# A two-layer encoder kernel on one core: layer 0's Fourier projection without the fold, q's norm moved into the masked minimum, roots by power, and another share of the PSUM banks

## The chip, the cores and the metric

The kernel runs on one core of a Trainium2 chip. The metric is the device time in microseconds (us) of one launch. The kernel before took 1091.9 us, the median of three runs (1090.97 to 1093.92).

## What is computed

Two layers over 512 positions of 1024 channels, in float32. Cut to what matters, each layer does this:

```python
h = rmsnorm(x, norm1[l])
p = h @ w_in[l]                       # columns: u (512) | q (8 x 64) | k (2 x 64) | v (2 x 64)
y_f = real(fft2(u, norm="ortho")) @ w_fourier[l] + b_fourier[l]
q = rope(rmsnorm(q, q_norm[l]));  k = rope(rmsnorm(k, k_norm[l]))
y_a = windowed_gqa(q, k, v, sink[l])  # |i - j| <= 128, a sink logit per head, blocks of 128 queries
x = x + concat(rmsnorm(y_f, g_fourier_out[l]), rmsnorm(y_a, g_attn_out[l])) @ w_o[l]
h = rmsnorm(x, norm2[l])
up = dwconv3(h @ w_up[l]);  gate, val = halves of up      # 2 x 2816 columns
x = x + (silu(gate) * val) @ w_down[l]
```

The real part of a two-dimensional Fourier transform is cosines over positions and channels less sines over both. Cosine columns are even and sine columns odd, so a transform of 512 points can be taken on sums and differences of mirrored points: 257 even values and 255 odd ones. This is called the fold here.

## The kernel before, in words

**Numbers.** Every float32 operand of a matmul is split into a high part, which ScalarE rounds, and a low part, the rest, which VectorE subtracts (`split`, L94, its lines L97 to L101 using the helpers L86, L89 and L92). A product is then three matmuls on TensorE (`mm3`, L106 to L108: high by high, low by high, high by low). x is held transposed, channels on partitions, in eight tiles `x` of 128 x 512.

**A layer's front.** `col_rstd` (L205) sums squares over the channels with eight small matmuls (L209, two columns wide) and calls `rsqrt` (L192): a shift and a subtraction for a first value and three Newton steps, twelve small VectorE operations (L196 to L202). The result r1 has one value for each position, on partitions. `row_rstd` (L212) spreads such values along rows with L216 (128 x 128 matmuls) and one ScalarE copy; the result is called rb.

- QKV: 2 groups x 8 channel tiles x 4 position blocks, each an `mm3` of 384 columns. Group 1 holds q's last pair of heads (called pair 3), k and v; group 0 holds q's pairs 0 to 2. The weights go through `wsplit` in layer 0; for layer 1 the split weights were prepared during layer 0's feed-forward part (`presplit`, L135) and come by DMA (`fetch`, L186). r1 is applied when the sums leave PSUM (L350 to L353).
- The Fourier projection: `fold_h` (L360) scales a tile of x by g and rb1 (L363), folds it (`fold`, L302: one copy of two columns, L304, and two operations of 255 columns) and splits it; in layer 0 `fold_wu` (L308) folds each weight tile too. 120 matmuls of 256 or 258 columns (L509 to L511) make the folded u in four PSUM banks.
- `prep` (L381) makes q and k ready: squares on ScalarE, a sum (L389), the root, a multiplication by the root (L397), rope in three multiplications and an addition, a split. Transposes by TensorE (L423, L434) turn them.
- Two stages of the transform (L529 to L559) with tables from `load_tables` (L272), each evacuated by `stage_out` (L518). The row for the Nyquist term is carried apart (`tail_out`, `altr`, L542 and L544).
- `attention(p)` (L445) for a pair of heads: in 8 blocks, scores into a bank tagged "sc" (L459), a VectorE operation that scales, adds the mask and finds the minimum (L463), an exponential on ScalarE, a reciprocal (L467), a multiplication on GpSimd (L468), transposes (L471), a split, and the products with v (`mm3`). Pair 3 comes first, then 0, then the Fourier output with `fold_wf` (L313) and its norm accF, then pairs 1 and 2.
- Wo in two halves: the first takes the normed Fourier output (`ys`) and is interleaved with attention's last blocks by `issue_after` (L615); the second takes attention's output with the norm accA. An attention's norm is applied to the sums (L636).

**The feed-forward part** is a long row of 512-column matmuls on TensorE, whose sums go through six banks in turn (`FFN_BANKS`).

**What sets the order.** The program is written in the order above, and a scheduler of the framework places the instructions of each engine's queue; a queue runs strictly in its order. Tiles come from rotating pools: a tag names a pool, and its count of buffers says how far a producer may be ahead (`TEMPS`, L72). The eight PSUM banks are shared out by tag (`BANKS`, L71): "mm" 3, "sc" 2, "tp" 2, "av" 1.

## Time and profile before

| | |
|---|---|
| median of three runs | 1091.9 us (1090.97 to 1093.92) |
| the profiled execution | 1089.6 us, its span 1087.8 us |
| granted TensorE clock | 0.995 of full |
| layer 0's front, up to attention's norm | 0 to 171 us |
| layer 0's rest and feed-forward part | to 564 us |
| layer 1's front, up to attention's norm | 564 to 700 us |
| VectorE, ScalarE, GpSimd over the span | 72%, 48%, 8% |

How to read the rows that follow: the page and the answers of the trace name engines PE (TensorE), PEld (its weight loads), DVE (VectorE), ACT (ScalarE), POOL (GpSimd) and SP (the queue that issues DMAs). L106 is line 106 of the kernel. A row of the timeline has the start, the duration, engine, line, operation, the tile written, an arrow and the tiles read, the shape and, behind x, how many of the kind were put together; in brackets stands the idle time before it and what ended it. Tiles whose name begins with ps are PSUM banks. TensorE's durations overlap, since a matmul begins while the one before drains.

### The profile page before, as it was taken

To read this page: it belongs to the slowest core of one execution; us is meant where nothing else is said; L and a number is where in the kernel's file an instruction comes from. 1 tells how busy PE (TensorE), PEld (TensorE's weight loads), DVE (VectorE), ACT (ScalarE), POOL (GpSimd) and SP (SyncE) were. 2 spreads that over 40 slices of the span, in tenths; PEclk is the share of its full clock that TensorE was granted. 3 is DMA by queue.
4 is the path that set the end of the run, shared out by engine and by line. 5 is a ranking of instruction groups with operands and counts; after the bars stand their busy time and mean duration, and the time that the engine had idled before them with its cause. 6 is when DMAs were issued, how large, how long until landed. Compare 5 with 4: busy or idle time off the path is not lost.

```text
span 1087.8 us, 14834 instructions
## 1 busy us (share of the span) xinstructions
PE 1058.9 (97%) x5187; PEld 889.0 (82%) x5187; DVE 785.0 (72%) x1574; ACT 522.4 (48%) x964; POOL 91.0 (8%) x158
## 2 busy tenths in 40 slices
PE   8987999999999999999999999999999999999998
PEld 7866878888888888888899887888888888888887
DVE  7898986787766777777628878386977435787632
ACT  5547863465444454545513676154554223454421
POOL 1014410000000000000000034000210000101000
PEclk9899999999999999999999999999999999999999
DMA  7312442333339943327855421422333333333241
GB/s 248 108 38 64 131 156 78 101 94 97 97 115 341 394 156 97 97 85 268 324 179 189 156 78 39 155 82 95 98 96 92 87 112 97 97 97 97 81 141 51
DMA packets 58573, 141.64 MB, mean 130 GB/s; under 512 B 6521, under 2 KB 19074, under 8 KB 58498
## 3 DMA queue, kind: packets, MB, share of 16 engines
q1 hardware_dynamic: 58498, 140.69, 40.1%
q8 instruction: 41, 0.67, 0.3%
q14 instruction: 34, 0.28, 0.1%
HBM read 117.60 MB, written 23.07 MB: 129 GB/s over the span
## 4 chain that ended last, share of the span: by engine, by line
PE 85%; DVE 10%; DMA 2%; ACT 2%; issue 2%; POOL 0%; SPq 0%; DVEq 0%; ACTq 0%; POOLq 0%
PE ps L106 27%; PE ps L108 27%; PE ps L107 27%; DVE tA L463 1%; DVE act L89 1%; DVE wlo L89 1%; DMA whi<-kept 1%; PE ps L471 1%; PE ps L459 1%; PE ps L216 1%; DVE tA L89 1%; ACT tA L86 1%; DVE tF L89 1%; PE ps L209 1%; DVE pT L89 0%
## 5 line engine op out<-in xcount | busy, mean ns | idle before, releaser
L86 ACT ACTIVATE whi<-wraw 128x512 fp32r<-128x512 f32 (+1 forms) x296 | 181.6, 616 | 290.9 <-PE ps L108 275.5
L106 PE MATMUL ps<-act,whi 128*128 128x512 f32 x768 | 298.9, 389 | 0.0
L107 PE MATMUL ps<-act,wlo 128*128 128x512 f32 x768 | 298.6, 390 | 0.0
L108 PE MATMUL ps<-act,whi 128*128 128x512 f32 x768 | 297.7, 389 | 0.0
L89 DVE TENSOR_TENSOR wlo<-wraw,whi 128x512 fp32r<-128x512 f32 (+1 forms) x304 | 218.7, 723 | 98.7 <-ACT whi L86 97.1
L108 PEld LDWEIGHTS ps<-act,whi 128*128 128x128 f32 x768 | 144.2, 188 | 29.9
L107 PEld LDWEIGHTS ps<-act,wlo 128*128 128x128 f32 x768 | 144.2, 188 | 29.9
L106 PEld LDWEIGHTS ps<-act,whi 128*128 128x128 f32 x768 | 144.2, 188 | 29.8
L92 DVE SCALAR_TENSOR_TENSOR tF<-tF,pb,tF 128x511 f32<-128x511 f32 x176 | 135.3, 772 | 10.7 <-ACT tF L86 8.0
L89 DVE TENSOR_TENSOR tF<-ps,rb 128x512 f32<-128x512 f32 x104 | 71.2, 689 | 77.2 <-PE ps L108 63.0
L106 PE MATMUL ps<-slab,whi 128*128 128x512 f32 (+2 forms) x228 | 86.7, 381 | 2.2 <-ACT whi L86 1.2
L107 PE MATMUL ps<-slab,wlo 128*128 128x512 f32 (+2 forms) x228 | 85.5, 375 | 0.0
L108 PE MATMUL ps<-slab,whi 128*128 128x512 f32 (+2 forms) x228 | 85.0, 375 | 0.0
L86 ACT ACTIVATE tF<-tF,pb 128x512 f32<-128x512 f32 x88 | 71.8, 816 | 12.0 <-DVE tF L89 3.9
L89 DVE TENSOR_TENSOR x<-x,ps 128x512 f32<-128x512 f32 (+1 forms) x49 | 32.8, 675 | 43.6 <-PE ps L108 43.4
L462 POOL COPY tA<-nsink 128x1 f32<-128x1 f32 x64 | 16.7, 265 | 489.4 <-DMA wraw<-in_w_down_dram 392.5
L89 POOL TENSOR_TENSOR tF<-tF,tF 128x512 f32<-128x512 f32 x22 | 30.2, 1374 | 316.2 <-DVE tF L92 309.2
L468 POOL TENSOR_SCALAR tA<-tA,den 128x256 f32<-128x256 f32 (+1 forms) x64 | 42.3, 665 | 130.9 <-DVE den L467 130.5
L106 PEld LDWEIGHTS ps<-slab,whi 128*128 128x128 f32 x228 | 42.8, 188 | 11.0 <-ACT whi L86 1.6
L107 PE MATMUL ps<-pT,wlo 128*128 128x512 f32 (+1 forms) x132 | 51.0, 386 | 0.0
L108 PE MATMUL ps<-pT,whi 128*128 128x512 f32 (+1 forms) x132 | 50.8, 385 | 0.0
L106 PE MATMUL ps<-pT,whi 128*128 128x512 f32 (+1 forms) x132 | 50.8, 385 | 0.0
(168 smaller groups left out, 1671.7 us busy)
## 6 DMA issues: line engine op xcount, KB each, us to landing
wraw<-in_w_up_dram SPq DMA_DIRECT2D x88, 512.0 KB, 3.5
wraw<-in_w_down_dram SPq DMA_DIRECT2D x32, 512.0 KB, 3.7
kept<-tA SPq DMA_DIRECT2D x56, 256.0 KB, 5.7
whi<-kept SPq DMA_DIRECT2D x28, 256.0 KB, 3.9
wlo<-kept SPq DMA_DIRECT2D x28, 256.0 KB, 2.7
kept<-tA SPq DMA_DIRECT2D x32, 192.0 KB, 2.1
wraw<-in_w_down_dram SPq DMA_DIRECT2D x32, 192.0 KB, 2.9
wraw<-in_w_o_dram SPq DMA_DIRECT2D x8, 512.0 KB, 5.2
```

The costliest lines, as they stand in the source:

```text
L86: return nc.scalar.activation(out, in_, func, **kw)
L89: return (eng or nc.vector).tensor_tensor(out, a, b, op=op)
L92: return nc.vector.scalar_tensor_tensor(out=out, in0=a, scalar=s, in1=b, op0=op0, op1=op1)
L106: nc.tensor.matmul(out, a[0], b[0], start=start, stop=False, **kw)
L107: nc.tensor.matmul(out, a[1], b[0], start=False, stop=False, **kw)
L108: nc.tensor.matmul(out, a[0], b[1], start=False, stop=stop, **kw)
L209: nc.tensor.matmul(pt[:, 2 * b:2 * b + 2], acc[:, b * P:(b + 1) * P], ones2, start=True, stop=True)
L216: nc.tensor.matmul(pt[:, b * P:(b + 1) * P], r[:, b:b + 1].to_broadcast([P, P]), ident, start=True, stop=True)
L459: nc.tensor.matmul(sc[:, :n], qT[p][:, e, i * P:(i + 1) * P], kT[g][:, s, j0 * P:(j1 + 1) * P], start=s == 0, stop=s == 1)
L462: nc.gpsimd.tensor_copy(pr[:, n:n + 1], nsink[:, l, h:h + 1])
L463: nc.vector.tensor_tensor_reduce(out=pr[:, :n], in0=sc[:, :n], in1=mask[:, m0:m0 + n], scale=-1.0 / math.sqrt(HD), scalar=nsink[:, l, h:h ...
L468: nc.gpsimd.tensor_scalar(pr[:, :n], pr[:, :n], den[:, i:i + 1], 1.0, op0=ALU.mult, op1=ALU.mult)
```

## The change

1. **Layer 0's u projection is not folded.** It uses the scaled and split x of QKV (`xg`), positions on partitions, and the weights as they are: 8 channel tiles x 4 position blocks x 3 = 96 matmuls of 512 columns. `fold_scaled` folds u over its channels when it leaves PSUM and applies r1. The fold over positions is left out: stage 0 sums over four blocks of 128 positions with four tables, the third and fourth being the first two with alternating signs, made on ScalarE. Layer 0 no longer calls `row_rstd(r1)`. Before the projection, in the program's order, stand the preparation of all q and attention 3.
2. **Layer 1 keeps the fold**, but `row_rstd(r1)` and the eight folds of x are written behind the preparation of k and of pair 3, not ahead of it.
3. **q's norm** no longer multiplies q: −r/8 of each query takes the place of the constant −1/8 in the scale of the masked minimum, so q's rope doesn't wait for the root.
4. **Roots**: `rsqrt` is one VectorE operation and one power (exponent −0.5) on GpSimd.
5. **Banks and buffers**: "mm" 4 and "sc" 1; "tA" 5 buffers instead of 6; the pool "sq" is gone and squares use "tF". Group 0 of QKV uses the banks sc, tp, tp and av, group 1 the four mm banks.
6. The tables and the folded Fourier weights are cut to 257 and 255 columns that start at a tile's edge (the odd part gets a first row of zeros), the tables come in five loads instead of two, half of each `w_fold` tile is loaded, and its sum and difference are written beside it.
7. In layer 0 attention 0 stands behind the Fourier output, with 1 and 2.

```diff
-FFN_BANKS = ("mm", "mm", "mm", "av", "sc", "sc")
+FFN_BANKS = ("mm", "mm", "mm", "mm", "av", "sc")
-    BANKS = {"mm": 3, "sc": 2, "tp": 2, "av": 1}
-             "tA": (512, 6), "tF": (512, 6), "sq": (512, 2)}
+    BANKS = {"mm": 4, "sc": 1, "tp": 2, "av": 1}
+             "tA": (512, 5), "tF": (512, 6)}
...
     def rsqrt(ssq, n, inv, tag, bufs=2):
         nc.vector.tensor_scalar(v, ssq, inv, EPS, op0=ALU.mult, op1=ALU.add)
-        nc.vector.tensor_scalar(it, v.bitcast(I32), 1, None, op0=ALU.logical_shift_right)
-        nc.vector.tensor_scalar(r.bitcast(I32), it, -1, float(0x5F3759DF), op0=ALU.mult, op1=ALU.add)
-        for _ in range(3):
-            tt(q, r, r, ALU.mult)
-            stt(q, q, -0.5, v, ALU.mult, ALU.mult)
-            stt(r, q, 1.5, r, ALU.add, ALU.mult)
+        nc.gpsimd.tensor_tensor(r, v, mhalf[:, :1].to_broadcast([P, n]), op=ALU.pow)
...
+    def fold_scaled(dst, src, scale):
+        up = temp(256, "tF")
+        act(up[:, :255], src[:, 257:512], scale=scale)
+        nc.vector.tensor_scalar(dst[:, 0:257:256], src[:, 0:257:256], scale, None, op0=ALU.mult)
+        stt(dst[:, 1:256], src[:, 1:256], scale, up[:, 254::-1], ALU.mult, ALU.add)
+        stt(dst[:, 257:512], src[:, 1:256], scale, up[:, 254::-1], ALU.mult, ALU.subtract)
...
         r1 = col_rstd(acc, 1.0 / D)
-        rb1 = row_rstd(r1)
         for grp in (1, 0):
-            pq = [psum("mm" if b < 3 else "av") for b in range(NB)]
+            pq = [psum("mm" if grp else ("sc", "tp", "tp", "av")[b]) for b in range(NB)]
...
-        for k in range(4):
-            fold_h(k)
...
+            nr = sp.tile([P, n, NB, 2], F32, tag=f"qknr{n}", name=nm("qknr"), bufs=1)
+            nc.vector.tensor_scalar(nr, r, -1.0 / math.sqrt(HD), None, op0=ALU.mult)
-                tt(t1, qraw[u], r[:, i, :, :, None].to_broadcast(shape), ALU.mult)
+                src = qraw[u]
+                if isk:
+                    src = t1
+                    tt(t1, qraw[u], r[:, i, :, :, None].to_broadcast(shape), ALU.mult)
+                else:
+                    qr[u] = nr[:, i]
...
-                        out=pr[:, :n], in0=sc[:, :n], in1=mask[:, m0:m0 + n], scale=-1.0 / math.sqrt(HD),
+                        out=pr[:, :n], in0=sc[:, :n], in1=mask[:, m0:m0 + n], scale=qr[p][:, i, e:e + 1],
...
+        if l == 0:
+            load_tables()
+            turn_rest()
+            attention(3, True)
+            pu = [psum() for _ in range(NB)]
+            for kk in range(KT // 2):
+                raw = load_wu(l, kk)
+                for k in (2 * kk, 2 * kk + 1):
+                    w = wsplit(raw[:, (k % 2) * 512:(k % 2 + 1) * 512])
+                    for b in range(NB):
+                        mm3(pu[b], [xg[k][:, s, b * P:(b + 1) * P] for s in range(2)], w, k == 0, k == KT - 1)
+            ub = []
+            for b in range(NB):
+                uf = temp(512, "tF")
+                fold_scaled(uf, pu[b], r1[:, b:b + 1])
+                a = pair("act")
+                split(a[:, 0, :], a[:, 1, :], uf)
+                ub.append(a)
+            ut = None
+        else:
+            rb1 = row_rstd(r1)
+            pe = [psum() for _ in range(3)]
+            po = psum("av")
+            for k in range(KT):
+                hr = temp(512, "tF")
+                stt(hr, x[k], g1[:, l, k:k + 1], rb1, ALU.mult, ALU.mult)
+                hf = fold(temp(512, "tF"), hr)
...
+        if l:
+            turn_rest()
+            attention(3, True)
...
-        for p in (1, 2):
+        for p in (1, 2) if l else range(3):
             attention(p, False)
```

The order of the instructions, as it was built, at three places. First VectorE's queue at r1's root in layer 0, before: nv, ni, nr and nq are the root's tiles, tl is the low part of a table, wraw a weight or table as loaded.

```order
43 L196 TENSOR_SCALAR nv_179<-ps_174 128x4 [waits PE_49]
44 L197 TENSOR_SCALAR ni_182<-nv_179 128x4 [waits DVE_49]
45 L198 TENSOR_SCALAR nr_180<-ni_182 128x4 [waits DVE_49]
46 L89 TENSOR_TENSOR nq_181<-nr_180 128x4 [waits DVE_49]
47 L92 SCALAR_TENSOR_TENSOR nq_181<-nq_181,nv_179 128x4 [waits DVE_49]
48 L92 SCALAR_TENSOR_TENSOR nr_180<-nq_181,nr_180 128x4 [waits DVE_49]
49 L89 TENSOR_TENSOR nq_181<-nr_180 128x4 [waits DVE_49]
50 L89 TENSOR_TENSOR tl_540<-wraw_537,th_539 128x512 [waits DMAHW5_49,Activation_49]
51 L92 SCALAR_TENSOR_TENSOR nq_181<-nq_181,nv_179 128x4 [waits DVE_49]
```

And the same place now, on VectorE:

```order
43 L89 TENSOR_TENSOR wlo_407<-wraw_404,whi_406 128x384 [waits DMAHW3_49,PE_49,Activation_49]
44 L89 TENSOR_TENSOR tl_560<-wraw_554,th_559 128x512 [waits DMAHW6_49,DMAHW7_49,DMAHW5_49,Activation_49]
45 L197 TENSOR_SCALAR nv_181<-ps_176 128x4 [waits PE_49]
46 L92 SCALAR_TENSOR_TENSOR vz_125<-ps_185,nr_182,vz_124 128x2x64 [waits Activation_49,Pool_49]
47 L92 SCALAR_TENSOR_TENSOR vz_125<-ps_186,nr_182,vz_124 128x2x64 [waits Activation_49]
48 L92 SCALAR_TENSOR_TENSOR vz_125<-ps_187,nr_182,vz_124 128x2x64 [waits Activation_49]
```

The root is one row there, and the table's split stands ahead of it. Second, TensorE's queue where the first scores of pair 3 stand in layer 0; before, they stand in stage 0 of the transform (slab is the folded u, th and tl the tables, m holds turned q and k):

```order
383 L106 MATMUL ps_1174<-slab_918,th_539 128x256 [waits DVE_49]
384 L107 MATMUL ps_1174<-slab_918,tl_540 128x256
385 L108 MATMUL ps_1174<-slab_918,th_539 128x256
386 L106 MATMUL ps_1174<-slab_923,th_545 128x256
387 L107 MATMUL ps_1174<-slab_923,tl_546 128x256
388 L459 MATMUL ps_1024<-m_105_595,m_110_620 128x256 [waits Activation_49]
389 L459 MATMUL ps_1024<-m_105_595,m_110_620 128x256
390 L459 MATMUL ps_1038<-m_105_595,m_110_620 128x384 x2
391 L108 MATMUL ps_1174<-slab_923,th_545 128x256 [waits DVE_49]
```

Now they stand right behind the u projection (act is the scaled x of QKV, whi and wlo the weights of u; L445 are transposes of q, L481 the scores):

```order
299 L106 MATMUL ps_814<-whi_936,act_170 128x512
300 L107 MATMUL ps_814<-whi_936,act_170 128x512
301 L108 MATMUL ps_814<-wlo_937,act_170 128x512
302 L106 MATMUL ps_815<-whi_936,act_170 128x512
303 L107 MATMUL ps_815<-whi_936,act_170 128x512
304 L108 MATMUL ps_815<-wlo_937,act_170 128x512
305 L481 MATMUL ps_665<-m_85_516,m_90_541 128x256 [waits Activation_49]
306 L481 MATMUL ps_665<-m_85_516,m_90_541 128x256
307 L445 MATMUL ps_623<-ident,m_103_605 128x128 [waits DVE_49,PE_49]
308 L445 MATMUL ps_623<-ident,m_103_605 128x128 x3
```

The scores moved ahead of both stages. Third, TensorE's queue in layer 1 at the spreading of r1, before (act is the scaled x, whi and wlo QKV's weights):

```order
2559 L106 MATMUL ps_5554<-whi_5654,act_5461 128x384 [waits DMAHW0_49,Activation_49]
2560 L107 MATMUL ps_5554<-whi_5654,act_5461 128x384
2561 L216 MATMUL ps_5547<-ident,nr_5532 128x128 [waits DVE_49,PE_49]
2562 L216 MATMUL ps_5547<-ident,nr_5532 128x128 x3
2563 L108 MATMUL ps_5554<-wlo_5655,act_5461 128x384 [waits DMAHW1_49]
2564 L106 MATMUL ps_5555<-whi_5654,act_5461 128x384
```

And now (slab is the folded x, the first operand of the u projection):

```order
2687 L212 MATMUL ps_5752<-ident,nr_5390 128x128 [waits Activation_49,Pool_49]
2688 L212 MATMUL ps_5752<-ident,nr_5390 128x128 x3
2689 L481 MATMUL ps_6133<-m_1230_5714,m_1235_5739 128x256 x2
2690 L481 MATMUL ps_6147<-m_1230_5714,m_1235_5739 128x384 [waits DVE_49]
2691 L481 MATMUL ps_6147<-m_1230_5714,m_1235_5739 128x384
...
2698 L445 MATMUL ps_6104<-ident,m_1302_6080 128x128 [waits Activation_49]
2699 L445 MATMUL ps_6104<-ident,m_1302_6080 128x128 x3
2700 L445 MATMUL ps_6110<-ident,m_1302_6080 128x128 [waits PE_49,Activation_49]
2701 L445 MATMUL ps_6110<-ident,m_1302_6080 128x128 x3
2702 L106 MATMUL ps_5759<-whi_5772,slab_5769 128x258 [waits DMAHW7_49,Activation_49]
2703 L106 MATMUL ps_5760<-whi_5772,slab_5769 128x258
```

It moved from within QKV to behind it and behind the transposes, and scores and more transposes stand between it and the u projection.

More of the change, by code (lines that the diff above doesn't have):

```diff
@@ L177, in presplit @@
             for i, key in enumerate(keys):
-                keep(key, prepare(key[0], got[i]))
+                src = got[i]
+                if key[0] == "u":
+                    src = fold(temp(512, "tA"), src)
+                keep(key, fold_w(src) if key[0] == "f" else src)
                 if i == len(keys) - 1 and n + 1 < len(jobs):
@@ L281, in load_tables, with add_square @@
         act(altr, alt)
-    def add_square(acc, src, first, tag="sq"):
+    def add_square(acc, src, first, tag="tF"):
         if first:
@@ L386, in prep @@
             for i, u in enumerate(us):
-                two = temp(1024, "act").rearrange("p (z b h d) -> p z b h d", z=2, **dims)
+                two = temp(1024, "act" if l else "slab").rearrange("p (z b h d) -> p z b h d", z=2, **dims)
                 act(two[:, 1], qraw[u], AF.Square)
@@ new lines, in encoder_kernel @@
+        pe = [psum() for _ in range(3)]
+        po = psum()
+        for m, (c0, c1) in enumerate(((0, 128), (128, 256), (256, 257))):
+            o = pe[m][:c1 - c0, :258]
+            for b, u2 in enumerate(ub):
+                mm3(o, [u2[:, s, c0:c1] for s in range(2)], [z[:, 0:258] for z in tab[b]],
+                    b == 0, ut is None and b == len(ub) - 1)
+            if ut is not None:
+                for s in range(2):
+                    nc.tensor.matmul(o, ut[:, s, c0:c1], altr, start=False, stop=s == 1)
@@ L566, in encoder_kernel @@
+        for m in range(2):
+            for i in range(2):
+                mm3(po[:, m * 256:(m + 1) * 256], [z[:, 256 + m * P:384 + m * P] for z in tab[i]],
+                    [ue[i][:, s, 256:512] for s in range(2)], m == 0 and i == 0, i == 1, skip_group_check=True)
+        ue, ut = stage_out(pe, po, 1.0 / 512.0)
+        if l:
+            attention(0, False)
         accF = accum("accF")
```

184 lines of the change are left out of this document (81 added, 103 removed).

## The prediction

> **What bounds the kernel now.** I read the page first, then the stretches of the two fronts (all that a layer does ahead of its feed-forward part), then the rows around the waits in them. The page's totals:
>
> ```profile
> PE 1058.9 (97%) x5187; PEld 889.0 (82%) x5187; DVE 785.0 (72%) x1574; ACT 522.4 (48%) x964; POOL 91.0 (8%) x158
> ```
>
> 97% says that TensorE sets the time as a whole. The change touches only the fronts, and there the table by stretch (time, then busy time of PE, PEld, DVE, ACT, POOL, granted clock, DMA share, GB/s) says something else:
>
> ```profile
> 30.00:49.00 19.00, 19.00 (x103) 18.92 (x101) 17.41 (x47) 9.97 (x22) 0.00 (x0) 0.90 0.40 115
> 49.00:82.00 33.00, 28.78 (x208) 24.02 (x207) 33.00 (x98) 17.47 (x37) 4.03 (x6) 1.00 0.16 51
> 82.00:145.00 63.00, 52.66 (x338) 43.90 (x336) 58.36 (x198) 50.30 (x137) 28.22 (x58) 0.97 0.30 95
> 594.00:610.00 16.00, 15.93 (x134) 14.89 (x135) 14.17 (x35) 9.69 (x19) 0.00 (x0) 1.00 0.84 284
> 610.00:666.00 56.00, 53.22 (x362) 45.04 (x360) 47.19 (x166) 43.38 (x120) 20.57 (x50) 1.00 0.18 55
> ```
>
> From 49 to 82 VectorE works in all of 33 us and from 82 to 145 in 58.36 of 63, while PE has gaps: layer 0's front is VectorE's. Layer 1's front (594 to 666) has VectorE at 61.4 of 72, and PE at 69.2. The places that I use, by PE's first row at each (layer 0: u projection, first scores, Wo's first half, attention's norm; layer 1: u projection, Wo's first half):
>
> ```profile
> 49.38 0.39 PE L106 MATMUL ps<-whi,slab 128*128 128x258 f32 x1
> ...
> 81.30 0.75 PE L459 MATMUL ps<-m,m 128*128 128x256 f32 x4
> ...
> 145.43 0.51 PE L106 MATMUL ps<-slab,whi 128*128 128x512 f32 x1 [0.31 <-ACT slab L86]
> ...
> 170.59 0.61 PE L209 MATMUL ps<-ones,acc 128*128 128x2 f32 x5
> ...
> 593.84 0.39 PE L106 MATMUL ps<-whi,slab 128*128 128x258 f32 x1
> ...
> 666.03 0.50 PE L106 MATMUL ps<-slab,whi 128*128 128x512 f32 x1 [0.40 <-ACT slab L86]
> ```
>
> PE's price is the distance of two starts, not a duration, since matmuls overlap: 595.46 − 595.34 = 0.12 us for 258 columns, 300.35 − 300.13 = 0.22 to 0.23 for 512.
>
> ```profile
> 595.34 0.28 PE L107 MATMUL ps<-whi,slab 128*128 128x258 f32 x1
> 595.46 0.28 PE L108 MATMUL ps<-wlo,slab 128*128 128x258 f32 x1
> ...
> 300.13 0.39 PE L106 MATMUL ps<-act,whi 128*128 128x512 f32 x1
> 300.35 0.39 PE L107 MATMUL ps<-act,wlo 128*128 128x512 f32 x1
> ```
>
> **Part 1: no wait for the row norm in layer 0's QKV.** VectorE starts r1's root at 25.33, is held in the middle by a table split that waited for its DMA, and ends the last step at 28.94 + 0.17; PE waits 4.50 us for that, spends 2.05 us on L216, and then runs 384-column matmuls 32.38 − 32.05 = 0.33 us apart instead of 36.94 − 36.77 = 0.17.
>
> ```profile
> 25.33 0.15 DVE L196 TENSOR_SCALAR nv<-ps 128x4 f32<-128x4 f32 x1
> ...
> 28.94 0.17 DVE L92 SCALAR_TENSOR_TENSOR nr<-nq,nr 128x4 f32<-128x4 f32 x1
> 29.25 2.05 PE L216 MATMUL ps<-ident,nr 128*128 128x128 f32 x8 [4.50 <-DVE nr L92]
> ...
> 32.05 0.52 PE L106 MATMUL ps<-whi,act 128*128 128x384 f32 x1
> 32.38 0.52 PE L107 MATMUL ps<-whi,act 128*128 128x384 f32 x1
> ...
> 36.77 0.33 PE L106 MATMUL ps<-whi,act 128*128 128x384 f32 x1
> 36.94 0.33 PE L107 MATMUL ps<-whi,act 128*128 128x384 f32 x1
> ```
>
> In the new order no L212 stands in this place, and the second group's sums have banks of their own, so PE needs r1 only when the u projection asks for "mm" banks. 4.50 + 2.05 and some nine slow matmuls at 0.15 are 7.9 us. The weights' splits must keep up, so I take 7: QKV ends at 42, not at 49.4. The Trainium skill, "TensorE: Matmul & The Clock Gate", section "HAM oscillation — how this bites in real kernels", says that idle gaps over about 3.4 us drop the clock to half; the 4.50 us gap followed by doubled spacing agrees. By it, a new gap that long in layer 1 would cost some 1.5 us more than itself.
>
> **Part 2: VectorE's work in layer 0.** Mean ns by group between 30 and 147 us:
>
> ```profile
> L92 DVE SCALAR_TENSOR_TENSOR tF<-x,pa,rb 128x512 f32<-128x512 f32 x8 | 6.0, 745 | 0.0
> ...
> L89 DVE TENSOR_TENSOR tF<-tF 128x255 f32<-128x255 f32 x16 | 6.2, 417 | 0.0
> ...
> L89 DVE TENSOR_TENSOR slab<-tF,slab 128x512 fp32r<-128x512 f32 x8 | 5.5, 685 | 0.0
> ...
> L89 DVE TENSOR_TENSOR tA<-wraw 128x255 f32<-128x255 f32 x16 | 6.3, 419 | 0.0
> ...
> L304 DVE COPY tF<-tF 128x2 f32<-128x2 f32 x8 | 1.3, 162 | 0.1
> ...
> L92 DVE SCALAR_TENSOR_TENSOR slab<-ps,slab 128x258 fp32r<-128x258 f32 x6 | 2.2, 409 | 0.0
> ...
> L89 DVE TENSOR_TENSOR act<-pT,qk3r 128x512 f32<-128x512 f32 x3 | 1.9, 672 | 0.0
> ...
> L92 DVE SCALAR_TENSOR_TENSOR qk3q<-qk3q,qk3v 128x24 f32<-128x24 f32 x3 | 0.5, 177 | 0.0
> ```
>
> Gone: eight scalings, folds and splits of x, 8 × (745 + 162 + 2 × 417 + 685) = 19.4 us; eight folds of w, 8 × (162 + 2 × 419) = 8.0; the evacuation of the folded u, 5 × 409 = 2.0; the multiplications of four q tiles by their root, 4 × 672 = 2.7; and in each of four roots eleven small operations of about 170, 7.5. Together 39.6. Added: four evacuations, each a small operation, two of 255 columns at 409 and a split of 685, 4 × 1.67 = 6.7, and two small scalings of −r/8. Net some 32.5 us of the 17.4 + 33.0 + 58.4 = 108.8 that VectorE is busy between 30 and 145.
>
> **Part 3: TensorE's work in layer 0** grows: 96 matmuls of 512 columns at 0.227 are 21.8 us where 120 at 0.12 were 14.3 (+7.5); stage 0 has 60 where 36 stood (24 × 0.12 = +2.9); L216 is gone (−2.05). That is +8.4 us, all on PE.
>
> **Part 4: the sum of layer 0.** From 42, the u projection takes 21.8 and some twenty transposes (0.11 each) 2.2; its weights need one split each, so PE is fed: first scores at 66, not 81.3. From there to Wo, VectorE's 58.4 lose the q preparation that now runs beside the projection (three reductions, six halves of rope, six full multiplications and three splits, by the rows above 10 to 11 us), three q multiplications (2.0) and most of two roots (3.4), and gain 5 to 7 of the new evacuations: 47. PE has to issue there about 48 us (156 matmuls of stage 0, stage 1 and the Fourier weights at 0.12 = 18.7; 27 of 32 score blocks, their transposes and the products of three pairs, some 27; two norms, 3). Two engines with 47 and 48 us that wait for each other: at the 93% that VectorE has in 82 to 145 they need 51 to 52, at the 85% that it has in layer 1's front (61.4 of 72) 56, and as far below that, at 79%, 61. I take 56: Wo starts at 122 to 123 instead of 145.4. But less has then been done: five score blocks and the last pair's products still lie there, 7 to 8 us of PE, so that the 25.2 us from 145.43 to 170.59 become 33. Attention's norm comes at 156, a gain of 14 to 15; with 61 us it is 9 to 10, with 51 it is 19 to 20. From there on the two kernels issue the same.
>
> **Part 5: roots by power.** The norm of the Fourier output is raised on VectorE from 134.69 to 141.19, twelve small steps between attention's work:
>
> ```profile
> 134.69 0.14 DVE L196 TENSOR_SCALAR nv<-ps 128x4 f32<-128x4 f32 x1
> ...
> 141.19 0.15 DVE L92 SCALAR_TENSOR_TENSOR nr<-nq,nr 128x4 f32<-128x4 f32 x1
> ```
>
> It becomes one VectorE step and one power on GpSimd, behind at most one of GpSimd's own operations. No row shows a power there; the nearest are these two:
>
> ```profile
> L462 POOL COPY tA<-nsink 128x1 f32<-128x1 f32 x64 | 16.7, 265 | 489.4 <-DMA wraw<-in_w_down_dram 392.5
> ...
> L89 POOL TENSOR_TENSOR tF<-tF,tF 128x512 f32<-128x512 f32 x22 | 30.2, 1374 | 316.2 <-DVE tF L92 309.2
> ```
>
> For 4 to 24 columns I take 0.5 us, between 0.27 and 1.4. Twelve calls at 1.4 are 11 us more than at 0.5, but only those for which PE waits count, four or five: 4 us at the most. The gain of about 4 us in each front's chain is in the 85% above.
>
> **Part 6: layer 1 pays.** There L216 stood inside QKV, so x was scaled, folded and split while PE multiplied; now L212 stands behind the transposes that follow QKV, and the eight folds come after it. First q's preparation for three tiles lies ahead of them on VectorE (about 10 us by the rows of part 2), then one scaling, fold and split (2.4): the u projection starts some 7 us late for PE, which has transposes and three score blocks to fill the rest. VectorE's work between QKV's end and Wo grows by 8 × 2.43 = 19.4, less what it had left of that at 594 (four splits), less the roots and q multiplications: about +8 on 61.4. At the pace of before (61.4 of 72 us) this is 81 us, +9; at 97% it is 72, no loss. Attention 3 now runs beside the projection and fills VectorE better than before: I take 90%, 77 us, +5 to +6.
>
> **Part 7: banks and buffers.** The score bank goes from two to one, "tA" from 6 to 5, the squares share "tF". PE used to issue scores while VectorE read the other bank:
>
> ```profile
> 103.12 0.47 DVE L463 CUSTOM_DVE_ANT_0 tA<-ps,pb,nsink 128x256 f32<-128x256 f32 x1
> ...
> 104.06 0.61 DVE L463 CUSTOM_DVE_ANT_0 tA<-ps,pb,nsink 128x384 f32<-128x384 f32 x1
> ...
> 104.07 0.51 PE L459 MATMUL ps<-m,act 128*128 128x384 f32 x2
> ```
>
> With one bank a block cannot come closer than L463 (0.47 to 0.61) plus the scores (0.51) plus two handovers (0.1 each or less), 1.2 to 1.3 us, where 0.94 was reached here. But layer 0 has 27 blocks in 56 us, 2.1 us each, so it costs only in the densest stretches: 2 us in all, between 0 and 0.3 for each of 64 blocks (19).
>
> Costed at nothing: eight more copies for the sign-changed tables on ScalarE, which has 9.97 us for 22 instructions in 30 to 49, 0.45 each, so 3.6 us in the 9 that it idles there (3.6 if the tables are late for stage 0, at 66 or later); three more loads on SP's queue ahead of the u weights, which have from about 30 to 42 to land while the DMA share is 0.40 (2 to 4 us if they don't); GpSimd's clearing of one table row, which waits for a buffer ahead of r1's power but has until 42; halved loads of the folded Fourier weights and their sums in place; and the feed-forward part's banks, six as before, where PE has no gaps.
>
> **The sum:** −14.5 + 5.5 + 2 = −7 us. The profiled execution took 1089.6 (span 1087.8), so it would take 1082.6. The median of before is 1091.9, 2.3 above it, and I forecast against that: 1085.
>
> **Rivals.**
> *Much more is gained* (14%): both engines run at 95% between first scores and Wo in layer 0, 5 to 6 us more, and layer 1's fuller VectorE takes its late folds in without loss, 5 more: 1074. For it speaks that PE and VectorE have nearly equal work there; against it, that no long stretch of the two fronts has VectorE and PE full at once.
> *It comes out even* (15%): layer 0 gains 9 (61 us in part 4), layer 1 loses 9 (pace of before): 1092. The extra 8.4 us of PE work is what makes this possible.
> *Layer 1 loses more than layer 0 gains* (10%): PE stands while q's preparation and each fold run on VectorE one after the other, with L481 of the next block queued ahead of the next fold's matmuls; at 2.4 us per fold plus 1.2 per interleaved block it loses 15, against 10 gained: 1097. It decides once the first u matmul is later than about 15 us behind QKV's end.
> *One score bank sets attention's pace* (14%): scores, minimum, scores, minimum in a chain, 64 × 0.3 = 19 us over both layers, against 9 gained without it: 1102. It decides above 9 / 64 = 0.14 us for each block. The Trainium skill, "PSUM — Partial Sum Buffer", section "Summary: rules for kernel authors", tells to read a bank only while the matmul writes to a different one, and this speaks against the change. The rows at 104.06 and 104.07 agree with how before did it.
>
> **How the numbers follow.** My own forecast has the other 47%. A measurement of this kernel tells 0.3%, 3.3 us, from no change. Faster by more: 47 + 14 = 61%; same 15%; slower 24%. The range leaves out about the outer half of the first and last rival: 1073 to 1101.
>
> **What would show it.** Right: no idle time of PE near 25 us; first scores near 66; Wo near 123 and accumulated attention norm near 156; in layer 1 some 5 to 8 us of new PE waits between QKV and the u projection, for VectorE's or ScalarE's slab, and Wo 5 to 6 us later relative to layer 0's end. Wrong: a power of several us on GpSimd, PE's waits for L485 at every block, a QKV held by weights or tables, or a u projection that waits for w.

## The result and the profile after

The changed kernel takes 1099.4 us (median of six runs, 1097.64 to 1102.01) against 1092.18 for the kernel before beside it: a ratio of 1.0071, 95% interval 1.0052 to 1.0089. It is slower by 0.7%. The forecast was 1085, faster; the stated range of 1073 to 1101 holds the measured time, but on the side that only the rivals led to. The profiled execution has a span of 1096.6 us, 8.8 more than before.

The page's totals, first. VectorE is busy 34 us less, as the change meant it to be, and TensorE 10 more:

```profile
PE 1068.5 (97%) x5179; PEld 898.5 (82%) x5179; DVE 751.3 (69%) x1394; ACT 521.9 (48%) x966; POOL 113.0 (10%) x171
```

The 10 us are not more work: a run below with the same matmuls and two score banks has TensorE busy for 1056.8 us, 2 less than before.

PE's first rows at the places that the prediction used, in the timeline of the changed kernel (QKV's end and the u projection, the first scores, Wo's first half, attention's norm; then the same in layer 1, with the spreading of r1, L212, ahead):

```profile
41.75 0.33 PE L108 MATMUL ps<-wlo,act 128*128 128x384 f32 x1
41.93 0.39 PE L106 MATMUL ps<-whi,act 128*128 128x512 f32 x1
...
66.63 0.40 PE L481 MATMUL ps<-m,m 128*128 128x256 f32 x2
...
137.78 0.50 PE L106 MATMUL ps<-slab,whi 128*128 128x512 f32 x1 [0.65 <-ACT slab L86]
...
173.18 0.61 PE L205 MATMUL ps<-ones,acc 128*128 128x2 f32 x5
...
594.04 1.13 PE L212 MATMUL ps<-ident,nr 128*128 128x128 f32 x8
...
603.28 0.74 PE L106 MATMUL ps<-whi,slab 128*128 128x258 f32 x4 [0.36 <-ACT slab L86]
...
711.76 0.61 PE L205 MATMUL ps<-ones,acc 128*128 128x2 f32 x5
```

Up to the first scores the kernel is 14.7 us ahead (66.6, where before had 81.3). From there to attention's norm it takes 106.6 us where before took 89.3, and all of the lead is gone: 173.2 against 170.6. Layer 1's front, from the sum of squares to attention's norm, takes 150.6 us (561.2 to 711.8) where before took 136.4 (564.0 to 700.4). The stretches behind each attention's norm, Wo's second half and the feed-forward part, gain 5.4 and 2.5. Together: −14.7 + 17.3 + 14.2 − 5.4 − 2.5 = +8.9, the 8.8 but for rounding.

The table by stretch (busy times of PE, PEld, DVE, ACT, POOL, then the granted clock) shows what kind of loss it is:

```profile
42.00:66.00 24.00, 24.00 (x119) 19.80 (x118) 22.23 (x52) 15.55 (x30) 4.61 (x1) 1.00 0.42 134
66.00:90.00 24.00, 20.57 (x110) 15.82 (x108) 18.41 (x64) 17.18 (x47) 7.52 (x22) 0.86 0.23 72
...
115.00:131.00 16.00, 12.65 (x61) 9.82 (x60) 13.94 (x45) 10.95 (x32) 5.55 (x12) 0.80 0.26 88
...
594.00:610.00 16.00, 12.65 (x86) 11.21 (x85) 16.00 (x44) 12.73 (x26) 10.55 (x6) 0.89 0.11 35
```

Through the u projection (42 to 66 us) PE is full and VectorE nearly. From the first scores on neither is: PE 20.57 and VectorE 18.41 of 24 us, and PE's clock falls to 0.86 and 0.80, where before had 1.00 from 49 to 82 us and 0.97 from 82 to 145. No engine bounds this stage; something makes them wait in turn. The last row, in layer 1, is another case: VectorE is busy for all of its 16 us, with the late folds among other work, and PE waits. The next two views show layer 0's waiting at one block. First VectorE's rows (L485 is the masked minimum, which reads the score bank):

```profile
76.87 0.53 DVE L485 CUSTOM_DVE_ANT_0 tA<-ps,pb,nsink 128x256 f32<-128x256 f32 x1
77.33 0.08 DVE L485 DVE_READ_ACCUMULATOR2_ANT nmax<- 128x1 f32 x1
77.33 0.16 DVE L489 RECIPROCAL den<-den 128x1 f32<-128x1 f32 x1
78.41 0.56 DVE L89 TENSOR_TENSOR pT<-ps,pT 128x384 fp32r<-128x384 f32 x1 [0.92 <-ACT pT L86]
78.88 0.67 DVE L485 CUSTOM_DVE_ANT_0 tA<-ps,pb,nsink 128x384 f32<-128x384 f32 x1
```

and PE's in the same 2 us:

```profile
77.01 0.84 PE L493 MATMUL ps<-ident,tA 128*128 128x128 f32 x3
77.50 0.56 PE L108 MATMUL ps<-pT,vz 128*128 128x256 f32 x1
77.86 0.84 PE L481 MATMUL ps<-m,m 128*128 128x384 f32 x2
```

The bank is free at 77.4. The next scores begin at 77.86, behind transposes and a product that stand ahead of them in PE's queue, and the next minimum at 78.88, behind a split that waited for ScalarE's copy of just those transposes. A block took 2.0 us, of which VectorE was busy 1.1. With one bank the scores cannot be issued before that bank has been read, so each engine's queue hangs on the same few blocks.

### The profile page after: what moved, and what is told of

Its sections match the earlier page's. It is cut to its first block, busy times and chain, and to the rows that moved or that the text cites. A ratio compares the mean times of both kernels' runs of the same rounds, so it can differ in the third digit from the quotient of the medians.

```text
span 1096.6 us, 14662 instructions
## 1 busy us (share of the span) xinstructions
PE 1068.5 (97%) x5179; PEld 898.5 (82%) x5179; DVE 751.3 (69%) x1394; ACT 521.9 (48%) x966; POOL 113.0 (10%) x171
## 4 chain that ended last, share of the span: by engine, by line
PE 91%; DVE 5%; ACT 1%; issue 1%; POOL 1%; DMA 0%; DVEq 0%; POOLq 0%; ACTq 0%
PE ps L106 29%; PE ps L108 29%; PE ps L107 29%; PE ps L493 1%; DVE tA L485 1%; PE ps L481 1%; DVE tF L92 1%; PE ps L205 1%; DVE pT L89 1%; ACT tA L86 0%; DVE act L89 0%; POOL tA L490 0%; PE ps L252 0%; DMA ropetab<-in_rope_dram 0%; ACT pT L86 0%
## 5 line engine op out<-in xcount | busy, mean ns | idle before, releaser
L86 ACT ACTIVATE whi<-wraw 128x512 fp32r<-128x512 f32 (+1 forms) x308 | 188.2, 616 | 278.8 <-PE ps L108 253.7
L89 DVE TENSOR_TENSOR wlo<-wraw,whi 128x512 fp32r<-128x512 f32 (+1 forms) x316 | 227.6, 723 | 101.9 <-ACT whi L86 98.8
L92 DVE SCALAR_TENSOR_TENSOR tF<-tF,pb,tF 128x511 f32<-128x511 f32 x176 | 133.1, 760 | 10.5 <-ACT tF L86 7.9
L106 PE MATMUL ps<-slab,whi 128*128 128x512 f32 (+2 forms) x228 | 85.6, 377 | 1.1 <-ACT slab L86 0.7
L108 PE MATMUL ps<-slab,whi 128*128 128x512 f32 (+2 forms) x228 | 83.2, 373 | 0.8 <-DVE slab L89 0.8
L107 PE MATMUL ps<-whi,act 128*128 128x384 f32 (+1 forms) x160 | 55.5, 350 | 0.0
L106 PE MATMUL ps<-whi,act 128*128 128x384 f32 (+1 forms) x160 | 54.5, 351 | 0.0
L484 POOL COPY tA<-nsink 128x1 f32<-128x1 f32 x64 | 14.1, 226 | 374.5 <-DVE tA L89 319.6
L108 PE MATMUL ps<-wlo,act 128*128 128x384 f32 (+1 forms) x160 | 50.7, 346 | 0.0
L106 PE MATMUL ps<-pT,whi 128*128 128x512 f32 (+1 forms) x132 | 50.5, 383 | 0.0
```

The costliest lines, as they stand in the source:

```text
L86: return nc.scalar.activation(out, in_, func, **kw)
L89: return (eng or nc.vector).tensor_tensor(out, a, b, op=op)
L92: return nc.vector.scalar_tensor_tensor(out=out, in0=a, scalar=s, in1=b, op0=op0, op1=op1)
L106: nc.tensor.matmul(out, a[0], b[0], start=start, stop=False, **kw)
L107: nc.tensor.matmul(out, a[1], b[0], start=False, stop=False, **kw)
L108: nc.tensor.matmul(out, a[0], b[1], start=False, stop=stop, **kw)
```

## The experiments

Times are medians, ratios against the kernel before beside them. Lines in the text are those of the changed kernel, unless before is named; rows of a run have the lines of its own kernel.

**One score bank in the kernel before.**

```diff
-    BANKS = {"mm": 3, "sc": 2, "tp": 2, "av": 1}
+    BANKS = {"mm": 4, "sc": 1, "tp": 2, "av": 1}
-            pe = [psum(), psum(), psum("sc")]
+            pe = [psum(), psum(), psum()]
```

(and the lists of banks for Wo and the feed-forward part as in the change.)

> The kernel before with one edit: the score banks go from two to one, the mm banks from three to four (the sums that used the second score bank take mm). One score bank as the cause: every block's scores wait for the minimum of the block before, so both fronts lengthen, by 5 to 10 us each, and the total by 10 to 19 us over before. Order of the work as the cause (layer 0's Fourier work can no longer run beside attention, layer 1's folds come late): within 3 us of before. A slow power: within 3 us of before.

1099.46 us, ratio 1.0079 (1.0065 to 1.0092): 8.2 over before. This one part, put into the old kernel, costs as much as the whole change does. It is less than the 10 to 19 us expected with one bank as the cause, and well over the 3 of the other two. Attention's norm in layer 0 comes 11.7 us later, at 182.3, although Wo's first half starts at 144.87, as early as before; attention ends last. Layer 1's front lost 3.3, less than expected of it, and a feed-forward part gained 2.9.

```profile
144.87 0.50 PE L106 MATMUL ps<-slab,whi 128*128 128x512 f32 x1
...
182.30 0.50 PE L209 MATMUL ps<-ones,acc 128*128 128x2 f32 x4
```

**Two score banks, at the cost of a transpose bank.**

```diff
-    BANKS = {"mm": 4, "sc": 1, "tp": 2, "av": 1}
+    BANKS = {"mm": 4, "sc": 2, "tp": 1, "av": 1}
-            pq = [psum("mm" if grp else ("sc", "tp", "tp", "av")[b]) for b in range(NB)]
+            pq = [psum("mm" if grp else ("sc", "sc", "tp", "av")[b]) for b in range(NB)]
```

> The changed kernel with two score banks again; the second comes from the transposes, which keep one. One score bank as the cause: the 71 us from the first scores to Wo in layer 0 fall to 60 to 65, layer 1's front from 150.6 to 143 to 147, total 8 to 15 us faster than the changed kernel's 1099 (1085 to 1091). Order as the cause: total within 3 us of 1099, or slower by some us, since transposes now wait for each other's evacuation.

1129.3 us, ratio 1.0352 (1.0335 to 1.0369), 30 slower than the changed kernel. It says nothing on the score bank, since the transposes took the loss (PE waits 19.4 us in all ahead of L445, L456 and L493, 9.0 ahead of the scores): this was a badly chosen experiment, and a warning that a bank is not spare because little time is spent in it.

**Layer 1's row norm and folds early again.**

```diff
         r1 = col_rstd(acc, 1.0 / D)
+        rb1 = row_rstd(r1) if l else None
...
+        if l:
+            for k in range(4):
+                fold_h(k)
         ra = sp.tile([P, 4, NB, HD], F32, tag="ropetab", name=nm("ropetab"), bufs=1)
```

> The changed kernel with layer 1's row norm and its first four folds of x written ahead of the preparation of k, as in before; everything else as changed. Late folds as the cause: layer 1's front (from the sum of squares to attention's norm) falls from 150.6 to 138 to 142 us, layer 0 stays, total 1087 to 1091. One score bank as the cause: the u projection starts earlier but attention is no shorter; front 147 to 150, total 1096 to 1099.

1091.94 us, ratio 1.0010 (1.0001 to 1.0018): 7.5 us faster than the changed kernel, within a microsecond of the 1087 to 1091 expected with the late folds as the cause, though layer 1's front of 146.0 us (561.9 to 707.9) lies between the two expectations for it. The u projection starts 28.5 us behind the sum of squares (561.9 to 590.40) instead of 42.1, 13.6 earlier, of which attention's norm kept 4.6 in the profiled execution. The late folds are a cause, and not the only one.

**Newton's steps again in the changed kernel.**

```diff
...
-        nc.gpsimd.tensor_tensor(r, v, mhalf[:, :1].to_broadcast([P, n]), op=ALU.pow)
+        nc.vector.tensor_scalar(it, v.bitcast(I32), 1, None, op0=ALU.logical_shift_right)
+        nc.vector.tensor_scalar(r.bitcast(I32), it, -1, float(0x5F3759DF), op0=ALU.mult, op1=ALU.add)
+        for _ in range(3):
+            tt(q, r, r, ALU.mult)
+            stt(q, q, -0.5, v, ALU.mult, ALU.mult)
+            stt(r, q, 1.5, r, ALU.add, ALU.mult)
```

> The changed kernel with the roots by Newton steps on VectorE again. A slow power (1.0 us for 4 columns, 3.0 to 4.4 for 16, 4.6 to 5.8 for 24) as a cause: 2 to 5 us faster, 1094 to 1097. Otherwise the power is beside other work and VectorE gets back some 2 us of small operations for each of twelve calls: 0 to 6 us slower, 1099 to 1105.

1103.14 us, ratio 1.0112 (1.0099 to 1.0125): 3.7 slower. The power is not the cause of the loss, though it is far from cheap.

**The banks of before in the changed kernel.**

```diff
-    BANKS = {"mm": 4, "sc": 1, "tp": 2, "av": 1}
+    BANKS = {"mm": 3, "sc": 2, "tp": 2, "av": 1}
-            pq = [psum("mm" if grp else ("sc", "tp", "tp", "av")[b]) for b in range(NB)]
+            pq = [psum((("mm", "mm", "mm", "av") if grp else ("sc", "sc", "tp", "tp"))[b]) for b in range(NB)]
-            attention(3, True)
-            pu = [psum() for _ in range(NB)]
+            pu = [psum("mm" if b < 3 else "av") for b in range(NB)]
...
+            attention(3, True)
             ut = None
         else:
```

(and the stages' third bank and the lists for Wo and the feed-forward part as in before.)

> The changed kernel with the banks of before: two score banks, three mm banks, the transposes keep their two; the u projection of layer 0 takes mm, mm, mm, av, so attention 3 is written behind it. One score bank as the cause: in layer 0 attention's first to last score fall from 90 us towards the 56 of before (60 to 72), attention's norm comes 6 to 12 us earlier than 173, and the total is 8 to 16 us under the changed kernel (1083 to 1091). If the score bank is not the cause, but that PE and VectorE wait in turn on a longer chain per block: within 4 us of 1099, attention still over 80 us.

1081.74 us, ratio 0.9915 (0.9901 to 0.9928): 17.7 us faster than the changed kernel, somewhat more than the 8 to 16 expected, and 9.5 faster than before. PE's first rows at the first scores, Wo and attention's norm:

```profile
66.19 0.75 PE L481 MATMUL ps<-m,m 128*128 128x256 f32 x4
...
125.23 0.50 PE L106 MATMUL ps<-slab,whi 128*128 128x512 f32 x1 [0.61 <-ACT slab L86]
...
160.28 0.72 PE L205 MATMUL ps<-ones,acc 128*128 128x2 f32 x6
```

They read 66, 125 and 160 where the forecast had 66, 123 and 156. The scores go out for two blocks at once (x4).

**The written order alone.** The run above had to move one more thing, attention 3 behind the u projection. So this move by itself, with the changed banks:

```diff
-            attention(3, True)
             pu = [psum() for _ in range(NB)]
...
+            attention(3, True)
             ut = None
```

> The changed kernel, its banks kept (one for scores, four mm), with one move: in layer 0 attention 3 is written behind the u projection, as it had to be in the kernel with the banks of before, which came to 1081.7. One score bank as the cause: 1095 to 1101, and attention in layer 0 still over 80 us from first to last score. The written order as the cause (attention 3 written first is preferred by the scheduler over stage 0, so that no Fourier matmuls stand beside it): 1081 to 1087, attention 70 to 75 us.

1097.3 us, ratio 1.0047 (1.0034 to 1.0061); its interval overlaps the changed kernel's, so the order alone gave 2.1 us by the medians, or nothing. The banks make the remaining 15.6. This pair of kernels, alike but for the banks, is the cleanest view of what a second score bank does. (The mm banks go from four to three with it, and some sums change banks; the score bank was not changed alone.) Stretches from 66 us on, with one bank:

```profile
66.00:131.00 65.00, 55.83 (x350) 47.03 (x350) 50.98 (x147) 42.88 (x111) 17.28 (x41) 0.92 0.14 44
131.00:156.00 25.00, 23.26 (x126) 19.27 (x124) 19.35 (x58) 14.94 (x40) 7.15 (x18) 1.00 0.27 85
```

and with two:

```profile
66.00:131.00 65.00, 59.02 (x400) 50.92 (x399) 54.47 (x173) 48.57 (x131) 22.50 (x52) 1.00 0.16 50
131.00:156.00 25.00, 25.00 (x131) 21.24 (x130) 18.86 (x45) 14.42 (x33) 4.17 (x8) 1.00 0.51 166
```

In the same 65 us TensorE gets through 400 instructions instead of 350, VectorE through 173 instead of 147, and the clock is 1.00 instead of 0.92. With one bank Wo's first half begins just as early and yet attention's norm comes 11.4 us later, because attention still has scores to issue at 154.79:

```profile
125.66 0.50 PE L106 MATMUL ps<-slab,whi 128*128 128x512 f32 x1
...
154.79 0.40 PE L481 MATMUL ps<-m,act 128*128 128x256 f32 x2
...
171.70 0.72 PE L205 MATMUL ps<-ones,acc 128*128 128x2 f32 x6
```

From first to last scores, layer 0's 32 blocks took 89 us with one bank (changed kernel 89.7, this one 89.2) and 71.5 with two. In this pair the bank set how long attention was; the order had moved what ran beside it. Other things set it too: a kernel with two score banks below, in which q is multiplied by its root, takes 78.4.

The starts and ends of the scores (L481), minima (L485) and transposes (L493) in the two traces show how. In layer 0, with one bank, the next block's scores start in the median 0.7 us after the minimum has freed the bank, held up by what stands ahead of them in PE's queue, and when a block's transposes begin, the scores of 1.5 later blocks have been issued on average. With two banks the next scores start 1.0 us before that minimum ends, and 4.0 later blocks have been issued. The distance of two blocks is 2.6 us in the median against 1.7. Two rows of the kernel with two banks, in which scores begin while VectorE still reads the other bank:

```profile
109.28 0.66 DVE L485 CUSTOM_DVE_ANT_0 tA<-ps,pb,nsink 128x384 f32<-128x384 f32 x1
...
109.84 0.40 PE L481 MATMUL ps<-m,act 128*128 128x256 f32 x2
```

**Both causes undone.** The banks of before and the early folds, two edits that stand above.

> The banks of before and layer 1's early row norm and folds in one kernel; what is left of the change is layer 0's unfolded projection, q's norm and the power. If the two causes add (early folds alone gave 7.5 us): 1076 to 1084, 8 to 16 under before. If both removed the same wait: as one of them, 1088 to 1092.

1073.87 us, ratio 0.9845 (0.9832 to 0.9859). That is 2 us below the 1076 to 1084 expected if the causes add. The early folds give 7.9 us beside two banks and gave 7.5 beside one: the causes do add. In layer 1 the u projection starts 28.5 us behind the sum of squares (549.3), not 39.9 as with late folds and two banks:

```profile
577.78 0.28 PE L106 MATMUL ps<-whi,slab 128*128 128x258 f32 x1
...
683.82 0.83 PE L205 MATMUL ps<-ones,acc 128*128 128x2 f32 x7
```

This kernel beats both: 17.4 us under before, 25.5 under the changed one. Five runs take one part at a time out of it or look at one alone.

**Attention 0 ahead of the Fourier output in layer 0**, as before wrote it:

```diff
-        if l:
-            attention(0, False)
+        attention(0, False)
-        for p in (1, 2) if l else range(3):
+        for p in (1, 2):
```

> As the kernel with the banks of before and the early folds, but in layer 0 attention 0 is written ahead of the Fourier output, as in before, not behind it. If the Fourier output's matmuls are needed as filler beside attention 0: 2 to 6 us slower than that kernel; if the order of the two sets nothing: within 1.5 us.

1076.46 us, ratio 0.9862 (0.9849 to 0.9876). The median is 2.6 us higher, but the interval overlaps that of the kernel without the edit: inconclusive.

**Newton's steps in it** (the edit shown above):

> The kernel with the banks of before and early folds (1073.9), with the roots by Newton steps on VectorE again. If the power pays in a front that VectorE bounds, as forecast: 3 to 8 us slower, 1077 to 1082. If its 3 to 6 us for 16 and 24 columns cost as much as they save, as in the kernel before with power and q's norm: within 3 us of 1073.9.

1082.21 us, ratio 0.9909 (0.9895 to 0.9923): 8.3 slower, just above the 3 to 8 that the forecast's reason gives. The power is worth 3.7 us in the changed kernel and 8.3 in this one, which has another order, early folds and two score banks; which of these makes the difference was not tried.

**Power and q's norm in the kernel before**, without the rest:

> The kernel before with two parts of the change: roots by power, and q's norm as the scale of the masked minimum. The forecast's pricing (VectorE loses about 20 us of small operations and 2.7 us of multiplications a layer in fronts that it bounds): 4 to 8 us faster than before, 1083 to 1087. If the power's 3 to 6 us for 16 and 24 columns stand in the chain to k, and so to the first scores: 2 to 6 us slower, 1093 to 1097.

1093.21 us, ratio 1.0018 (1.0008 to 1.0028): no gain, 2 us lost. Its edits are items 3 and 4 of the change. The longest wait of PE in it was 6.7 us, at 64.5 us, for the split of a folded x, which stands behind q's sums and rope in VectorE's queue (58.91 to 63.76); in before that wait was 1.7. It was made good, though: the first scores stand at 81.28, as in before (81.30), and attention's norm 7.2 us later (177.8), so layer 0's loss lies between the two. So the same parts that pay in the unfolded front did not pay in the folded one. Which of the two parts lost there was not tried.

**q multiplied by its root again**, in the best kernel:

```diff
-                src = qraw[u]
-                if isk:
-                    src = t1
-                    tt(t1, qraw[u], r[:, i, :, :, None].to_broadcast(shape), ALU.mult)
-                else:
-                    qr[u] = nr[:, i]
+                src = t1
+                tt(t1, qraw[u], r[:, i, :, :, None].to_broadcast(shape), ALU.mult)
...
-                        out=pr[:, :n], in0=sc[:, :n], in1=mask[:, m0:m0 + n], scale=qr[p][:, i, e:e + 1],
+                        out=pr[:, :n], in0=sc[:, :n], in1=mask[:, m0:m0 + n], scale=-1.0 / math.sqrt(HD),
```

> The kernel with the banks of before and early folds, with q multiplied by its root again and the constant scale in the masked minimum. Forecast's pricing (four multiplications of 0.67 us a layer on VectorE, 2.7 us): 2 to 6 us slower, 1076 to 1080. If only the count matters off the path: within 1.5 us. If q then waits for the power of 24 columns (4.6 to 5.8 us) ahead of its rope: more than 6 us slower.

1080.17 us, ratio 0.9899 (0.9885 to 0.9912): 6.3 slower, at the border of two expectations; the multiplications alone are 5.4 us over both layers, and q's rope then waits for a power of 24 columns as well. In the profiled executions all of it lies in layer 0: attention's norm comes 5.3 us later there (166.6 against 161.3), while layer 1's front is 0.9 shorter. How much is the multiplications and how much the wait for the power is not settled.

**Layer 0's projection folded again**, in the best kernel: `row_rstd(r1)` and `fold_h` for both layers, weights folded, two tables, attention 0 and 3 at the places of layer 1:

```diff
+                    w = wsplit(fold(temp(512, "tA"), raw0[:, (k % 2) * 512:(k % 2 + 1) * 512]))
-                        mm3(pu[b], [xg[k][:, s, b * P:(b + 1) * P] for s in range(2)], w, k == 0, k == KT - 1)
```

> The kernel with the banks of before and early folds (1073.9), with layer 0's projection folded as in before (row norm, folds of x and of the weights, 120 matmuls of 258 columns, two tables); power, q's norm and the rest as changed. If the unfolded projection is worth what the forecast gave it (14 to 15 us of layer 0's front): 1085 to 1092, first scores near 80 instead of 67. If the gain of that kernel comes from its other parts: 1072 to 1078.

1091.99 us, ratio 1.0003 (0.9992 to 1.0014): 18.1 slower than with the unfolded projection, and no different from before. Its row norm is back in QKV, and its first scores stand at 86.23:

```profile
29.79 1.16 PE L212 MATMUL ps<-ident,nr 128*128 128x128 f32 x8
...
86.23 0.40 PE L487 MATMUL ps<-m,m 128*128 128x256 f32 x2
```

Attention's norm in layer 0 comes 14.0 us later (175.2 against 161.3). So the unfolded projection makes most of the gain; the places of attention 0 (2.6 us, not clear of noise, in the run above) and attention 3 are in the 18.1 too. TensorE is as busy with either (1056.7 us folded, 1056.5 unfolded), and VectorE 19 us less with the unfolded one (766.8 against 748.0).

## Why the prediction was wrong, step by step

- **Part 1, right in the number, with one cause too many.** The idle time near 25 us is gone and the u projection begins at 41.93; 42 was forecast. But the run with the folded projection keeps the row norm inside QKV (L212 at 29.79), PE does not wait for it, and its QKV ends at 42.2 as well. The power without the new banks (in the kernel before) left QKV's end at 48.4. So leaving out the row norm was not needed; this points to the second group's own banks, which the part names too.
- **Parts 2 to 4 up to the first scores, right.** They begin at 66.6; 66 was forecast. Against the best kernel with the fold, its removal (and the places of attention 0 and 3) is worth 14.0 us of layer 0's front and 18.1 as a whole. Against before, that front gained 10.3 us with two score banks (170.6 to 160.3), where part 4 had 14 to 15.
- **Part 4, the pace behind the scores, wrong for this kernel and 5 us short for one with two score banks.** The step "two engines with 47 and 48 us that wait for each other", at 85%, gave 56 us from the first scores to Wo, and 33 more to attention's norm: 89. It took 106.6. With the banks of before it took 94.1 (59.0 and 35.1). With one bank and the order of that run it took 106.0, though Wo began after 60.0: so the order sets where Wo begins (after 71.2 in the changed kernel), and the bank how much of attention is then left. The pace had been read from a kernel whose attention had two score banks, and was carried over to one that had a single bank.
- **Part 5, mis-sized, with the right sign.** The power was bounded by rows of other operations at 0.27 to 1.4 us whatever its columns. It takes 1.0 us for 4 columns and 3.0 to 5.8 for 16 and 24 (rows in the last section). Its use is still worth 3.7 us here and 8.3 in the best kernel.
- **Part 6, right in kind, too small.** 5 to 6 us were forecast, 7.5 and 7.9 were measured. The first u matmul stands 14.7 us behind QKV's last (588.59 to 603.28), and the clock is 0.89 from 594 to 610. PE idles for 5.2 us of the gap, within the forecast's 5 to 8, but it waits there for the k and q tiles that it transposes and for a score block's minimum more than for the folded x. "Some 7 us late" had left out that two score blocks' minima (596.46 and 599.39) stand ahead of the first fold (600.07) on VectorE, and scores and transposes ahead of the first u matmul on PE.
- **Part 7 is the term that failed: 2 us forecast, 15.6 measured** (the run with the order alone against the one with the banks too), or 17.7 with the order, over 64 blocks some 0.24 to 0.28 each. The step that failed is the one from a closest spacing of 1.2 to 1.3 us, with 2.1 us there for each block, to "it costs only in the densest stretches". It compared an average spacing with a shortest one. Attention's blocks do not come evenly, since they depend on k, q and the products of the pair before, and the scores stand behind other rows in a queue that is strictly in order. With one bank the next scores wait for every one of these; two banks let one block be late; this is read from the rows, not tried engine by engine. Taken from the rows: 2.0 us for a block in the stretch shown above, where PE has no Fourier work yet; the forecast had 1.2 to 1.3 as the closest. The other things that the part names, one buffer less of "tA" and the squares in "tF", were not tried apart; the best kernel still has them.

With 15.6 in the place of 2 and 7.7 in the place of 5.5 the forecast's own sum is −14.5 + 7.7 + 15.6 = +9 us, 1101; measured were 1099.4. That it comes so near is partly luck: layer 0's front gained 10.3 rather than 14.5 with two banks, and the 5.4 behind attention's norm in layer 0 were in no term. The rival "one score bank sets attention's pace" had this cause, at 19 us and 1102, with a chance of 14%. Its bare chain of scores and minimum is not quite what the rows show: PE stands waiting for a minimum only 7 times in the changed kernel's 64 blocks, 5.1 us in all, and otherwise the next scores stand behind other rows of the same chain. The rule that was cited for it, the Trainium skill, "PSUM — Partial Sum Buffer", section "Summary: rules for kernel authors", to read a bank only while the matmul writes to a different one, weighed against the change. With one score bank the kernel can keep it only by holding the next scores back, and the banks made 15.6 us here. The clock took part: 0.92 from 66 to 131 us with one bank against 1.00 with two. By that row it took at most 0.08 × 65 = 5.2 us of TensorE's time, an estimate, of the 11.4 that layer 0's front lost; the rest, 6 us at the least, is waiting. The Trainium skill, "TensorE: Matmul & The Clock Gate", section "A second HAM failure mode: psum-queue depth-cycling", describes, for bf16 matmuls of 512 columns, short gaps of TensorE between groups, as it cycles through PSUM banks, that make the clock swing. The changed kernel's matmuls are others, but where its clock was 0.86 and 0.80 TensorE idled for 3.4 of 24 and 3.4 of 16 us; that these gaps lowered the clock was not tested.

The 7.9 us that the stretches behind attention's norm gained (Wo's second half and the feed-forward parts, 5.4 + 2.5) were not forecast. Layer 0's feed-forward part was 2.9 shorter in the old kernel with the new banks as well, and 3.2 shorter in the best kernel, which has the old ones, so the banks alone do not explain it; it stays open.

## What to carry to other kernels

Before a PSUM bank is moved from one use to another, look at what reads it: here a bank whose reader is in a chain over several in-order queues needed a second one although its average spacing looked ample. A pace read from a profile belongs to the buffers that it was measured with; where the change takes buffers away, price the chain with every engine's queue in order, not the busy times. And a bundle of edits is worth taking apart: here one part cost 16 to 18 us, one 8, and the rest gained 17, so that the bundle lost and the rest alone won.

## What the runs showed that was not expected

The power on GpSimd costs by the column: 0.2 to 0.3 us for each of 4 to 24 columns on 128 partitions, by the groups of the changed kernel (in a shape the number behind 128x is the columns; behind the bar stand the busy time in us and the mean of one in ns):

```profile
L198 POOL TENSOR_TENSOR qk3r<-qk3v,mhalf 128x24 f32<-128x24 f32 x2 | 10.4, 5204 | 31.9 <-DVE qk3v L197 31.9
L198 POOL TENSOR_TENSOR nr<-nv,mhalf 128x4 f32<-128x4 f32 x8 | 8.9, 1110 | 135.7 <-DVE nv L197 135.7
L198 POOL TENSOR_TENSOR qk2r<-qk2v,mhalf 128x16 f32<-128x16 f32 x2 | 7.4, 3708 | 20.9 <-DVE qk2v L197 20.9
```

A transposition bank taken away (two to one) and given to the scores cost 30 us, twice what the score bank was worth.
